# One decoder layer on one core: the first head's inputs loaded at once, the norm vector spread by TensorE, first products taken by kind, statistics on ScalarE alone

## The chip, the cores and the metric

The kernel runs on one core of a Trainium2 chip. The metric is the device time of one execution in microseconds, lower is better. A time is the median of several executions; the profile shows one execution more.

## What is computed

One layer of a hybrid decoder in fp32: 16 meta tokens ahead of 1024 tokens of width 1024, a norm, one projection into the inputs of two head groups (differential attention and a gated recurrence), an output projection, and a feed-forward part with a convolution. Cut to what the change touches:

```python
h = jnp.concatenate([meta, x], axis=1)            # 16 + 1024 rows of 1024
a = rmsnorm(h, ln_mix_pre[l])                     # h * rsqrt(mean(h*h) + eps) * gain
proj = a @ w_in[l]                                # 1024 -> 7 * 512 columns
dq, dk, dv, hq, hf, hi, hg = jnp.split(proj, SPLITS, axis=-1)
y_diff = diff_attention(dq, dk, dv, ...)          # 4 heads
y_hgrn = hgrn2(hq, hf, hi, hg, ...)               # 4 heads
mix = jnp.concatenate([y_diff, y_hgrn], axis=-1) @ w_out[l]
h = h + rmsnorm(mix, ln_mix_post[l])
h = h + rmsnorm(conv_ffn(rmsnorm(h, ln_ffn_pre[l]), ...), ln_ffn_post[l])
```

## The kernel before

**Tiling.** The 1040 rows are nine blocks: block 0 holds the 16 meta rows, blocks 1 to 8 hold 128 rows each. Three blocks make a group; group 0 is blocks 0 to 2 (272 rows), groups 1 and 2 have 384 rows. Each block is cut into two halves of 512 columns (half 0 and 1), which are the first and last four of the eight contraction steps of the projection.

**A product in three passes.** Each fp32 operand is split into a rounded high part and the rest: the activations into `ahi` and `alo`, the weights into `wh` and `wl`. A product of one contraction step is three matmuls, `wh`·`ahi`, `wh`·`alo`, `wl`·`ahi` (`proj_step`, lines 222, 224, 226), into one PSUM bank. `dq`, `dk` and `dv` are the three weight tiles of the first attention head; their results are `pi_dq`, `pi_dk`, `pi_dv`. dv's two weight halves are split into tiles that the rows call `w` (VectorE's cast and GpSimd's rest lie in one tile).

**The path of a block.** `load_x` loads `xt`. `pre_stat` gets the sum of squares with a Square and its accumulator, then Ln and Exp on ScalarE make the factor `ss`. `pre_scale` multiplies one half by `ss` and the gain `gb` on VectorE into `xs`. `pre_turn` turns it with four transposes on TensorE into PSUM (`px`). `pre_hi` casts `px` into `ahi` on ScalarE, `pre_lo` subtracts on VectorE into `alo`. `weights` splits a weight half (`wr`): a cast on ScalarE into `wh`, a subtraction on GpSimd into `wl`. In the profile all of ScalarE's and VectorE's operations carry line 53, that of the wrapper `Ordered`; tile names tell them apart.

**Order.** TensorE's queue is in the order of the code. While `state["ordered"]` is true ScalarE and VectorE keep the code's order too; after that a scheduler orders them. The loads go through one queue, SP's. A tile's readers and writers wait for each other through semaphores per tile: two halves in one tile are one thing to these waits. PSUM tiles have a tag: `ip` and `m` have two banks each, `S` has two tiles of two banks. `interleave` feeds a stretch of products with pieces of side work, here the blocks 3 to 5 (`pre_blocks`), which belong to group 1, between the products of group 0; `lead` and `fill` set how many products (counted in ns) go between the pieces.

**The front before.** `gb`'s first half is made by a matmul with a row of ones and copied; its second half is loaded with the row repeated for every partition. Statistics of block 0 are VectorE's, their squares go to PSUM (`pj`). Group 0's products begin as soon as half 0 of the three blocks is cast, each contraction step with all three kinds. `dv`'s weights are loaded when buffers come free. `pi_dv` takes a bank of `ip`, which `pi_dq` and `pi_dk` have had.

Of the kernel before, what the change touches and what calls it, by code (L numbers as in the profile page):

```python
# [13 lines left out]
ALU = mybir.AluOpType  # L14
# [71 lines left out]
def layer_kernel(ctx: ExitStack, tc: tile.TileContext, x, meta, table, lbl, gpre, gpost, win,  # L86
# [148 lines left out]
    xts = {}  # L235

    def load_x(i):
        xts[i] = zp.tile([P, D], F32, tag="xt", name=f"xt{i}", bufs=4)
# [12 lines left out]

    def pre_scale(i, half, ss, xs):
        r = rows(i)
        cs = slice(512 * half, 512 * half + 512)
        V.scalar_tensor_tensor(xs[:r, :512], xts[i][:r, cs], ss[:r], gb[:r, cs], ALU.mult, ALU.mult)

    def pre_turn(i, half, xs, pt=None):
        r = rows(i)
        pt = ps_m(f"px{i}_{half}") if pt is None else pt
        for j in range(4):  # L260
            T.transpose(pt[:, j * r:(j + 1) * r], xs[:r, P * j: P * (j + 1)], ident[:r, :r])
# [494 lines left out]
    parts = []  # L756
    grow = zp.tile([P, D], F32, tag="xt", name="grow", bufs=4)[:1]
# [5 lines left out]
    def load_raw(m, c, name):  # L763
        raw = wp.tile([P, 512], F32, tag="wr", name=f"wr_{name}_{c}", bufs=3)
        SY.dma_start(raw, win[m][:, 512 * c: 512 * (c + 1)])
        return raw

    def split_raw(raw, name):
        hi = wp.tile([P, 512], F32R, tag="wh", name=f"wh_{name}", bufs=4)
        lo = wp.tile([P, 512], F32R, tag="wl", name=f"wl_{name}", bufs=4)  # L770
        split(hi, lo, raw)
        return hi, lo

    raws = {}
# [6 lines left out]
    stat = {0: pre_stat(0)}  # L781
    pt = ps_m("pg")
    T.matmul(pt, ones, grow[:, :512], start=True, stop=True)
    V.tensor_copy(gb[:, :512], pt)
    load_x(3)
    xss = {}
    for i in range(3):
        for half in range(2):
            if i < 2 and half == 1:
                xss[i, 1] = xss[i, 0][:, 512:]  # L790
            elif i < 2:
                xss[i, 0] = zp.tile([P, D], F32, tag="xs", name=f"xs{i}")
            else:
                xss[i, half] = ap_.tile([P, 4, P], F32, tag="at0", name=f"xs{i}_{half}", bufs=2).rearrange("p a c -> p (a c)")
    parts = [[None, None], [None, None]]

    def weights(j, c):
        parts[j][c] = split_raw(raws[j, c], f"{tiles[j][1]}_{c}")

    def scale(i, half):  # L800
        pre_scale(i, half, stat[i], xss[i, half])

    spare = {}

    def turn(i, half):
        if i and i not in spare:
            spare[i] = ps_s(f"px{i}")
        return pre_turn(i, half, xss[i, half], spare[i][:, half] if i else None)

    stat[1] = pre_stat(1)  # L810
    scale(0, 0)
    h00 = turn(0, 0)
    stat[2] = pre_stat(2)
    scale(1, 0)
    h10 = turn(1, 0)
    scale(0, 1)
    h01 = turn(0, 1)
    pre_hi(*h00)
    weights(0, 0)
    raws[1, 1] = load_raw(tiles[1][0], 1, tiles[1][1])  # L820
    load_x(4)
    scale(2, 0)
    h20 = turn(2, 0)
    pre_lo(*h00)
    pre_hi(*h10)
    scale(1, 1)
    h11 = turn(1, 1)
    load_x(5)
    pre_lo(*h10)
    pre_hi(*h20)  # L830
    weights(1, 0)
    scale(2, 1)
    pre_lo(*h20)
    pre_hi(*h01)
    pre_lo(*h01)
    weights(0, 1)
    pre_hi(*h11)
    pre_lo(*h11)
    for i in range(3):
        xts.pop(i)  # L840

    def head0_first():
# [4 lines left out]
        for half in range(2):  # L847
            for j in range(2):
                for k in range(4 * half, 4 * half + 4):
                    yield from proj_step(pts[j], parts[j], k, t0, t1, lambda: tiles[j][2](0, *g0, t0, t1, pts[j]))  # L850
        yield from proj_group(0, parts[2], tiles[2][1], tiles[2][2])

    first_group = head0_first()
    for _ in range(3):
        next(first_group)
    h21 = turn(2, 1)
    last_hi = pre_hi(*h21)
    last_lo = pre_lo(*h21)
    weights(1, 1)
    state["ordered"] = False  # L860
    third = [ap_.tile([P, 4, 512], F32R, tag="pb", name=f"w3{c}", bufs=2) for c in range(2)]
    parts.append([])
# [715 lines left out]
```

## Time and profile before

| | |
|---|---|
| median of 3 runs | 1347.83 us (1342.91 to 1348.17) |
| the profiled execution | 1345.7 us, its span 1343.9 us |
| TensorE busy | 1290.4 us (96%) |
| VectorE, ScalarE, GpSimd busy | 910.7, 690.6, 429.7 us |
| loads and stores | 165.26 MB, mean 123 GB/s |

A row of the timeline is: start, duration, engine, line, operation, out<-in, shape, count, and in brackets the idle time ahead of it with what ended it. Times of start are counted from the span's start. A row of a stretch is: its ends, its length, then busy time and count of TensorE, its weight loads, VectorE, ScalarE and GpSimd, the granted TensorE clock, the share of the DMA engines, and GB/s.

### The profile page before, as it was taken

The numbers are of one execution on the slowest core, as the hardware profiler recorded it, in microseconds if no ns is written. First come the engines' busy times: TensorE is split into PE (matmuls) and PEld (weight loads), VectorE is DVE, ScalarE is ACT, GpSimd is POOL, SyncE is SP. The second block draws the span as 40 slices with busy tenths as digits, with TensorE's granted clock in tenths as the row PEclk, the third lists the DMA queues.
The fourth block names the chain that finished last, engine by engine and source line by source line (L and its number), as shares of the span: only waits on it lengthen the run. The fifth ranks groups of instructions, "written<-read, shape, count | busy, mean of one in ns | idle before, by whom it ended". The sixth has DMA issues, their size and how long they took to land.

```text
span 1343.9 us, 26160 instructions
## 1 busy us (share of the span) xinstructions
PE 1290.4 (96%) x10170; PEld 1189.0 (88%) x10170; DVE 910.7 (68%) x1535; ACT 690.6 (51%) x1631; POOL 429.7 (32%) x334
## 2 busy tenths in 40 slices
PE   6999999999999998999999999999999999999997
PEld 5899899989999998687899999999999998888875
DVE  7665647574756474636798777787777776697586
ACT  7465356535754666236674444454454444454453
POOL 3211211121102110326046657657656640010121
PEclk9999999999999999999999999999999999999999
DMA  6342334143311223667512222223222225965263
GB/s 214 109 135 67 115 110 150 64 139 117 127 48 53 79 87 114 201 184 251 204 48 87 87 79 80 80 86 104 80 87 77 74 89 187 340 192 159 92 203 118
DMA packets 99570, 165.26 MB, mean 123 GB/s; under 512 B 10051, under 2 KB 34915, under 8 KB 99446
## 3 DMA queue, kind: packets, MB, share of 16 engines
q1 hardware_dynamic: 99446, 163.58, 37.1%
q8 instruction: 80, 1.31, 0.4%
q14 instruction: 44, 0.36, 0.1%
HBM read 122.91 MB, written 40.63 MB: 122 GB/s over the span
## 4 chain that ended last, share of the span: by engine, by line
PE 47%; DVE 5%; DMA 3%; ACT 3%; issue 3%; POOL 2%; SPq 0%; DVEq 0%; ACTq 0%; POOLq 0%
PE pd L1424 5%; PE pd L1423 5%; PE pd L1425 5%; PE pb L1265 4%; PE pb L1266 4%; PE pb L1267 4%; PE pc L1265 2%; PE pa L1265 2%; PE pc L1267 2%; PE pa L1267 2%; PE pa L1266 2%; PE pc L1266 2%; PE py L945 1%; PE py L941 1%; PE py L943 1%
## 5 line engine op out<-in xcount | busy, mean ns | idle before, releaser
L1265 PE MATMUL pb<-t,uh 128*128 128x258 f32 x504 | 143.8, 285 | 5.7 <-DVE u L53 5.7
L1266 PE MATMUL pb<-t,uh 128*128 128x258 f32 x504 | 142.6, 283 | 0.0
L1267 PE MATMUL pb<-t,ul 128*128 128x258 f32 x504 | 142.3, 282 | 0.0
L1424 PE MATMUL pd<-wl,gh 128*128 128x512 f32 x308 | 121.9, 396 | 0.1
L1423 PE MATMUL pd<-wh,gh 128*128 128x512 f32 x308 | 121.7, 395 | 0.0
L1425 PE MATMUL pd<-wh,gl 128*128 128x512 f32 x308 | 121.7, 395 | 0.0
L53 DVE SCALAR_TENSOR_TENSOR c<-uu,cwt,c 128x514 f32<-128x514 f32 (+1 forms) x88 | 96.8, 1100 | 20.6 <-ACT c L53 19.9
L1232 POOL TENSOR_TENSOR c<-c,c 128x514 f32<-128x514 f32 (+1 forms) x44 | 63.5, 1443 | 121.9 <-ACT c L53 119.2
L1265 PEld LDWEIGHTS pb<-t,uh 128*128 128x128 f32 x504 | 96.1, 191 | 7.1 <-DVE u L53 6.9
L1266 PEld LDWEIGHTS pb<-t,uh 128*128 128x128 f32 x504 | 96.1, 191 | 0.0
L1267 PEld LDWEIGHTS pb<-t,ul 128*128 128x128 f32 x504 | 95.9, 190 | 0.0
L1265 PE MATMUL pa<-t,uh 128*128 128x258 f32 (+1 forms) x336 | 95.3, 284 | 0.0
L1266 PE MATMUL pa<-t,uh 128*128 128x258 f32 (+1 forms) x336 | 95.1, 283 | 0.0
L1267 PE MATMUL pa<-t,ul 128*128 128x258 f32 (+1 forms) x336 | 95.0, 283 | 0.0
L1265 PE MATMUL pc<-t,uh 128*128 128x258 f32 (+1 forms) x336 | 94.0, 280 | 0.0
L1267 PE MATMUL pc<-t,ul 128*128 128x258 f32 (+1 forms) x336 | 93.9, 280 | 0.0
L1266 PE MATMUL pc<-t,uh 128*128 128x258 f32 (+1 forms) x336 | 93.7, 279 | 0.0
L53 DVE SCALAR_TENSOR_TENSOR c<-ug,cwt,c 128x514 f32<-128x514 f32 (+1 forms) x88 | 86.1, 978 | 2.7 <-ACT c L53 2.0
L147 POOL TENSOR_TENSOR ul<-ws,uh 128x512 fp32r<-128x512 f32 x42 | 61.1, 1454 | 42.8 <-ACT uh L53 38.3
L1424 PEld LDWEIGHTS pd<-wl,gh 128*128 128x128 f32 x308 | 57.7, 187 | 14.9 <-DVE wl L53 0.9
L1425 PEld LDWEIGHTS pd<-wh,gl 128*128 128x128 f32 x308 | 57.7, 187 | 14.1
L1423 PEld LDWEIGHTS pd<-wh,gh 128*128 128x128 f32 x308 | 57.7, 187 | 14.1
(349 smaller groups left out, 4131.1 us busy)
## 6 DMA issues: line engine op xcount, KB each, us to landing
ra<-in_wup_dram SPq DMA_DIRECT2D x88, 256.0 KB, 2.7
mp<-msc SPq DMA_DIRECT2D x23, 512.0 KB, 5.4
wd<-in_wdown_dram SPq DMA_DIRECT2D x44, 256.0 KB, 4.4
tsc<-wd SPq DMA_DIRECT2D x44, 256.0 KB, 3.2
wi<-tsc SPq DMA_DIRECT2D x44, 256.0 KB, 2.8
gi<-gsc SPq DMA_DIRECT2D x33, 256.0 KB, 4.2
wi<-in_wdown_dram SPq DMA_DIRECT2D x33, 256.0 KB, 3.0
gsc<-c SPq DMA_DIRECT2D x22, 257.0 KB, 2.1
```

Source lines behind the costliest of these rows:

```text
L53: ins = call(*args, **kw)
L147: (eng or G).tensor_tensor(lo, raw, hi.bitcast(F32), op=ALU.subtract)
L941: T.matmul(py[:r], mh, hi, start=(first and k == ks[0]), stop=False)
L943: T.matmul(py[:r], mh, lo, start=False, stop=False)
L945: T.matmul(py[:r], ml, hi, start=False, stop=(last and k == ks[-1]))
L1232: G.tensor_tensor(cg, cg, cu, op=ALU.mult)
L1265: T.matmul(pt, hi[:, s], th[:, k], start=(first and k == 0), stop=False, skip_group_check=True)
L1266: T.matmul(pt, hi[:, s], tl[:, k], start=False, stop=False, skip_group_check=True)
L1267: T.matmul(pt, lo[:, s], th[:, k], start=False, stop=(k == 3), skip_group_check=True)
L1423: T.matmul(py, gh[:, s], wh, start=(k == 0 and pr not in (3, 7)), stop=False, skip_group_check=True)
L1424: T.matmul(py, gh[:, s], wl, start=False, stop=False, skip_group_check=True)
L1425: T.matmul(py, gl[:, s], wh, start=False, stop=(k == NH - 1), skip_group_check=True)
```

## The change

All is in the first stretch of the program.

- **Loads.** All of the first head's inputs are issued at once, ahead of any wait for a buffer: three tiles that are first used much later (`X0`, `X1`, `X2`) take blocks 2 to 5, the fourth half of dq and dk and both halves of dv. `gb`'s repeated load is gone: the whole row is loaded once.
- **Norm vector.** Both halves of `gb` are made by a matmul with ones and a copy.
- **Statistics.** ScalarE squares all blocks, block 0 too; the squares go to `xs` in SBUF instead of PSUM, and `xs` is then overwritten by the scaling.
- **Turns.** Blocks 1 to 8 have both halves in one two-bank `S` tile (before, blocks 3 to 8 had a bank of `m` for each half).
- **Products by kind.** `head0_first` takes the products of dq and dk kind by kind: four steps of `wh`·`ahi` for dq, four for dk, then `wl`·`ahi`, `wh`·`alo`, and so on. `pi_dv` takes a bank of `m`.
- **Interleaving.** `interleave(first_group, ..., 800, 3500)` becomes `(450, 4900)`.

```diff
     def pre_stat(i):
         r = rows(i)
-        junk = ps_s(f"pj{i}").rearrange("p a c -> p (a c)")
+        xss[i] = zp.tile([P, D], F32, tag="xs", name=f"xs{i}", bufs=3)
         ss = zp.tile([P, 1], F32, tag="ss", name=f"ss{i}", bufs=3)
-        if i == 0:
-            V.scalar_tensor_tensor(junk[:r], xts[i][:r], 1.0, xts[i][:r], ALU.mult, ALU.mult, accum_out=ss[:r])
-        else:
-            A.activation(junk[:r], xts[i][:r], AF.Square, accum_out=ss[:r])
+        A.activation(xss[i][:r], xts[i][:r], AF.Square, accum_out=ss[:r])
         rstd_of(ss[:r], ss[:r], D)
...
     def pre_block(i):
         with tc.issue_after(last_hi.ins):
             ss = pre_stat(i)
-        xs = zp.tile([P, D], F32, tag="xs", name=f"xs{i}")
         for half in range(2):
-            pre_scale(i, half, ss, xs[:, 512 * half:])
-        xts.pop(i)
+            pre_scale(i, half, ss)
+        pt = ps_s(f"px{i}")
         for half in range(2):
-            out_ = pre_turn(i, half, xs[:, 512 * half:])
+            out_ = pre_turn(i, half, pt[:, half])
             pre_hi(*out_)
             pre_lo(*out_)
             yield
...
-    SY.dma_start(grow[:, :512], gpre[:, :512])
-    for i in range(3):
-        load_x(i)
-    SY.dma_start(gb[:, 512:], gpre[:, 512:].to_broadcast([P, 512]))
+    SY.dma_start(grow, gpre)
+    spare = [spare_tile(t) for t in ("X1", "X2", "X0")]
+    load_x(0)
+    load_x(1)
+    load_x(2, spare[2][:, :D])
...
     for c in range(2):
         for j in range(2):
-            if (j, c) != (1, 1):
-                raws[j, c] = load_raw(tiles[j][0], c, tiles[j][1])
+            load_raw(j, c)
+    load_x(3, spare[1][:, :D])
+    for c in range(2):
+        load_raw(2, c)
+    load_x(4, spare[1][:, D:2 * D])
+    load_x(5, spare[2][:, D:2 * D])
...
+    for half in range(2):
+        cs = slice(512 * half, 512 * half + 512)
+        pt = ps_m(f"pg{half}")
+        T.matmul(pt, ones, grow[:, cs], start=True, stop=True)
+        V.tensor_copy(gb[:, cs], pt)
+        if half == 0:
+            pre_scale(0, 0, stat[0])
...
+        yield from part(0, 0, 0, ahi, True)
+        yield from part(1, 0, 0, ahi, True)
+        yield from part(0, 0, 1, ahi)
+        yield from part(0, 0, 0, alo)
...
+        pts.append(ps_m("pi_dv0_0")[:, :n])
...
-    interleave(first_group, [pre_blocks([3, 4, 5])], 800, 3500)
+    interleave(first_group, [pre_blocks([3, 4, 5])], 450, 4900)
```

What it moves is seen in the order of the instructions. First, the start of TensorE's queue. Before (`px_173` is block 1, `px_194` block 2, `px_0_162` and `px_1_179` the two halves of block 0):

```order
L783 MATMUL pg<-grow,ones 128x512
L261 MATMUL px_0_162<-ident,xs_152 128x16 x4
L261 MATMUL px_173<-ident,xs_153 128x128 x4
L261 MATMUL px_1_179<-ident,xs_152 128x16 x4
L261 MATMUL px_194<-ident,xs_0_154 128x128 x4
L261 MATMUL px_173<-ident,xs_153 128x128 x4
L222 MATMUL pi_dq_0_224<-ahi,wh_dq_0_185 128x272
L224 MATMUL pi_dq_0_224<-alo,wh_dq_0_185 128x272
L226 MATMUL pi_dq_0_224<-ahi,wl_dq_0_186 128x272
L261 MATMUL px_194<-ident,xs_1_155 128x128 x4
```

And now (`px_175` is block 1, `px_176` block 2):

```order
L796 MATMUL pg_164<-grow,ones 128x512
L796 MATMUL pg_168<-grow,ones 128x512
L261 MATMUL px_0_173<-ident,xs_149 128x16 x4
L261 MATMUL px_175<-ident,xs_154 128x128 x8
L261 MATMUL px_176<-ident,xs_159 128x128 x8
L837 MATMUL pi_dq_0_228<-ahi,wh_dq_0_204 128x272 x4
L837 MATMUL pi_dk_0_229<-ahi,wh_dk_0_212 128x272 x2
L261 MATMUL px_1_174<-ident,xs_149 128x16 x4
L837 MATMUL pi_dk_0_229<-ahi,wh_dk_0_212 128x272 x2
L837 MATMUL pi_dq_0_228<-ahi,wl_dq_0_205 128x272 x4
L837 MATMUL pi_dq_0_228<-alo,wh_dq_0_204 128x272 x4
```

The second norm product and the wide turns of both halves have moved ahead of the first product, and eight products with high parts alone stand ahead of the first with `alo`.

Second, TensorE's queue in the dv products, with the semaphores that a row waits for (DVE, Activation, PE and Pool are those of VectorE, ScalarE, TensorE and GpSimd). Now (`px_311` is block 3, `px_341` block 4; the second group of each name is half 1):

```order
L222 MATMUL pi_dv_0_302<-ahi,w_244 128x272 [waits DVE_49,PE_49]
L261 MATMUL px_311<-ident,xs_304 128x128 [waits DVE_49,PE_49]
...
L261 MATMUL px_311<-ident,xs_304 128x128 [waits DVE_49]
...
L261 MATMUL px_341<-ident,xs_334 128x128 [waits PE_49,Activation_49]
...
L261 MATMUL px_341<-ident,xs_334 128x128 [waits DVE_49]
```

Before, with the halves of block 4 in tiles of their own (`px_0_336` and `px_1_351`):

```order
L261 MATMUL px_0_336<-ident,xs_333 128x128 x4
L222 MATMUL pi_dv_0_343<-ahi,w_239 128x272
L224 MATMUL pi_dv_0_343<-alo,w_239 128x272
L226 MATMUL pi_dv_0_343<-ahi,w_239 128x272
...
L261 MATMUL px_1_351<-ident,xs_333 128x128 x4
L224 MATMUL pi_dv_0_343<-alo,w_239 128x272
```

All six groups of turns of blocks 3 to 5 now stand between dv's products, four apart, where before the first of them stood among dq's and dk's and the later ones seven apart; and the second half of a block is turned into the tile from which VectorE reads the first half for `alo`.

Third, ScalarE around the evacuation of `pi_dq` and `pi_dk` (`q`, `k`). Before, with `px_0_288` and `px_1_306` block 3:

```order
L53 CAST ahi<-px_0_288 128x4x128
L53 ACTIVATE q_0_120<-pi_dq_0_224 64x272
L53 ACTIVATE pj_439,ss_440<-xt_326 128x1024
L53 CAST ahi<-px_1_306 128x4x128
L53 ACTIVATE q_0_121<-pi_dq_0_224 64x272
L53 CAST k_0_122<-pi_dk_0_225 64x272
L53 CAST ahi<-px_0_336 128x4x128
```

And now:

```order
L53 ACTIVATE q_0_120<-pi_dq_0_228 64x272
L53 ACTIVATE xs_362,ss_363<-X_in 128x1024
L53 CAST k_0_122<-pi_dk_0_229 64x272
L53 ACTIVATE q_0_121<-pi_dq_0_228 64x272
L53 CAST ahi<-px_311 128x4x128
L53 ACTIVATE ss_363<-ss_363,eps 128x1
```

Block 3's first cast now comes behind the evacuations and a Square, where before it came ahead of them.

More of the change, by code (lines that the diff above doesn't have):

```diff
@@ L787, in layer_kernel @@
-    for i in range(3):
-        for half in range(2):
[L789 to L798, printed above, removed]
@@ L831, in layer_kernel, with turn @@
+    turned = {}
+    def turn(i, half):
+        turned[i, half] = pre_turn(i, half, banks0[i][half])
+    for i in (1, 2):
+        for half in range(2):
+            pre_scale(i, half, stat[i])
+    pre_scale(0, 1, stat[0])
+    for i, half in ((0, 0), (1, 0), (1, 1), (2, 0), (2, 1)):
+        turn(i, half)
+    pre_hi(*turned[0, 0])
+    pre_hi(*turned[1, 0])
+    weights(0, 0)
+    pre_hi(*turned[2, 0])
+    for i in range(3):
+        pre_lo(*turned[i, 0])
     weights(1, 0)
-    scale(2, 1)
@@ L833, in layer_kernel @@
-    pre_lo(*h20)
-    pre_hi(*h01)
-    pre_lo(*h01)
+    pre_hi(*turned[1, 1])
     weights(0, 1)
[L837 to L840, printed above, removed]
+    last_hi = pre_hi(*turned[2, 1])
+    weights(1, 1)
+    load_x(7)
     def head0_first():
@@ L846, in head0_first, with part @@
         pts = [ps_in(f"pi_{tiles[j][1]}_0")[:, :n] for j in range(2)]
[L847 to L851, printed above, removed]
+        def part(j, half, w, a, first=False, last=False):
+            for k in range(4 * half, 4 * half + 4):
+                T.matmul(pts[j], parts[j][half][w][:, P * (k % 4): P * (k % 4 + 1)], a[:, k, t0:t1],
+                         start=(first and k == 0), stop=(last and k == KD - 1))
+                if last and k == KD - 1:
+                    tiles[j][2](0, *g0, t0, t1, pts[j])
+                yield 115
@@ L853, in layer_kernel @@
+        pts.append(ps_m("pi_dv0_0")[:, :n])
+        for k in range(KD):
+            yield from proj_step(pts[2], parts[2], k, t0, t1, lambda: tiles[2][2](0, *g0, t0, t1, pts[2]))
     first_group = head0_first()
-    for _ in range(3):
+    for _ in range(6):
         next(first_group)
[L856 to L859, printed above, removed]
+    turn(0, 1)
+    pre_hi(*turned[0, 1])
+    for i in range(3):
+        last_lo = pre_lo(*turned[i, 1])
     state["ordered"] = False
```

106 lines of the change are left out of this document (45 added, 61 removed).

## The prediction

> **What bounds the kernel now.** I read the busy times of the page, then a table of stretches cut where TensorE starts and stops waiting, then the timelines of the first 33 us.
>
> ```profile
> span 1343.9 us, 26160 instructions
> PE 1290.4 (96%) x10170; PEld 1189.0 (88%) x10170; DVE 910.7 (68%) x1535; ACT 690.6 (51%) x1631; POOL 429.7 (32%) x334
> ```
>
> TensorE is busy 96% of the span, so only a stretch in which it idles or runs slowly can give time back. The stretches (TensorE's busy time comes first behind the length):
>
> ```profile
> 2.18:11.48 9.30, 6.13 (x23) 3.61 (x23) 5.51 (x9) 5.53 (x15) 3.61 (x6) 1.00 0.87 286
> 11.48:24.55 13.07, 9.73 (x62) 9.04 (x62) 9.55 (x13) 9.16 (x23) 7.32 (x6) 1.00 0.58 191
> 24.55:32.68 8.13, 5.60 (x44) 4.92 (x42) 7.87 (x18) 7.38 (x21) 0.00 (x0) 1.00 0.74 245
> 32.68:49.13 16.45, 16.45 (x100) 15.50 (x101) 10.40 (x27) 7.85 (x19) 0.00 (x0) 1.00 0.01 2
> ```
>
> From 32.68 us TensorE runs 16.45 us without a gap. The change ends ahead of there: what it is worth is how much earlier that unbroken run begins. TensorE's timeline before it:
>
> ```profile
> 2.18 2.04 PE L783 MATMUL pg<-grow,ones 1*128 1x512 f32 x2 [2.18 <-DMA grow<-in_gpre_dram]
> ...
> 7.71 1.11 PE L261 MATMUL px<-ident,xs 128*128 128x128 f32 x4 [1.08 <-DVE xs L53]
> ...
> 11.48 0.60 PE L222 MATMUL pi_dq<-ahi,wh_dq 128*128 128x272 f32 x1
> 14.49 0.60 PE L224 MATMUL pi_dq<-alo,wh_dq 128*128 128x272 f32 x1 [2.42 <-DVE alo L53]
> ...
> 15.11 1.06 PE L261 MATMUL px<-ident,xs 128*128 128x128 f32 x4
> 15.82 0.58 PE L222 MATMUL pi_dq<-ahi,wh_dq 128*128 128x272 f32 x1
> ...
> 17.32 0.42 PE L222 MATMUL pi_dq<-ahi,wh_dq 128*128 128x272 f32 x1
> 17.55 0.33 PE L224 MATMUL pi_dq<-alo,wh_dq 128*128 128x272 f32 x1
> 17.72 0.29 PE L226 MATMUL pi_dq<-ahi,wl_dq 128*128 128x272 f32 x1
> 17.84 0.29 PE L222 MATMUL pi_dk<-ahi,wh_dk 128*128 128x272 f32 x1
> ...
> 21.50 0.63 PE L261 MATMUL px<-ident,xs 128*128 128x128 f32 x4 [0.72 <-DVE xs L53]
> ...
> 24.55 0.60 PE L261 MATMUL px<-ident,xs 128*128 128x128 f32 x4
> 26.85 0.37 PE L222 MATMUL pi_dv<-ahi,w 128*128 128x272 f32 x1 [1.71 <-DVE q L53]
> 27.05 0.29 PE L224 MATMUL pi_dv<-alo,w 128*128 128x272 f32 x1
> ...
> 31.95 0.44 PE L222 MATMUL pi_dq<-ahi,wh_dq 128*128 128x384 f32 x1 [0.54 <-ACT ahi L53]
> 32.68 0.44 PE L224 MATMUL pi_dq<-alo,wh_dq 128*128 128x384 f32 x1 [0.28 <-DVE alo L53]
> 32.95 0.34 PE L226 MATMUL pi_dq<-ahi,wl_dq 128*128 128x384 f32 x1
> 33.13 0.34 PE L222 MATMUL pi_dq<-ahi,wh_dq 128*128 128x384 f32 x1
> ```
>
> Three losses are to be seen. The second product waits until 14.49 for alo. Products start 0.23 us apart up to 17.55 and 0.12 apart from 17.72, so TensorE is slow at first; it sped up 3.06 us after its unbroken run began at 14.49 (the table's clock column reads 1.00 throughout and does not show it). And dv waits 1.71 us for its bank, which dq holds. Taking 0.17 us for the product at 31.95, the unbroken run in effect begins at 32.5.
>
> **The change part by part.** The rows that price the start, on ScalarE, VectorE, GpSimd and the load queue:
>
> ```profile
> 4.60 0.29 ACT L53 ACTIVATE ss<-ss,eps 16x1 f32<-16x1 f32 x1 [2.59 <-DVE pj L53]
> ...
> 5.16 1.03 ACT L53 ACTIVATE pj<-xt 128x1024 f32<-128x1024 f32 x1
> 6.12 0.19 ACT L53 ACTIVATION_READ_ACCUMULATOR pj<-xt 128x1 f32 x1
> ...
> 6.78 1.01 ACT L53 ACTIVATE pj<-xt 128x1024 f32<-128x1024 f32 x1
> ...
> 8.87 0.62 ACT L53 CAST wh_dq<-wr_dq 128x512 fp32r<-128x512 f32 x1 [0.30 <-DMA wr_dq<-in_win_dram]
> 9.39 0.58 ACT L53 CAST ahi<-px 128x512 fp32r<-128x512 f32 x1
> ...
> 22.16 0.59 ACT L53 CAST ahi<-px 128x512 fp32r<-128x512 f32 x1 [0.70 <-PE px L261]
> ```
>
> ```profile
> 3.22 1.22 DVE L53 SCALAR_TENSOR_TENSOR pj<-xt 16x1024 f32<-16x1024 f32 x1 [3.22 <-DMA xt<-in_meta_dram]
> 4.37 0.67 DVE L53 COPY gb<-pg 128x512 f32<-128x512 f32 x1
> ...
> 8.23 1.40 DVE L53 SCALAR_TENSOR_TENSOR xs<-xt,ss,gb 16x512 f32<-16x512 f32 x2 [0.57 <-DMA gb<-in_gpre_dram]
> ...
> 11.76 0.69 DVE L53 TENSOR_TENSOR alo<-px,ahi 128x512 fp32r<-128x512 f32 x1 [1.34 <-PE px L261]
> ...
> 19.49 1.20 DVE L53 CAST w<-wr 128x512 fp32r<-128x512 f32 x1 [0.46 <-DMA wr<-in_win_dram]
> 20.61 3.10 DVE L53 SCALAR_TENSOR_TENSOR xs<-xt,ss,gb 128x512 f32<-128x512 f32 x3
> ...
> 24.82 1.41 DVE L53 SCALAR_TENSOR_TENSOR xs<-xt,ss,gb 128x512 f32<-128x512 f32 x2
> ```
>
> ```profile
> 12.02 1.27 POOL L147 TENSOR_TENSOR wl_dk<-wr_dk,wh_dk 128x512 fp32r<-128x512 f32 x1 [0.46 <-ACT wh_dk L53]
> ```
>
> ```profile
> 11.58 0.33 SPq L765 DMA_DIRECT2D wr_dk<-in_win_dram  x1
> ```
>
> *Statistics on ScalarE.* The meta rows are there at 3.2. A Square and its read take about 1.2, so the first Ln starts at 4.4 instead of 4.60, and with 1.62 a block (5.16 to 6.78) block 2's factor is there at 8.15, 0.3 us sooner. A Square into SBUF has no row here; the casts bound its extra cost between 0 and 0.04 (0.58 out of PSUM, 0.62 out of SBUF). I take 0. The Trainium skill, page "ScalarE: Activation LUTs", section "Step-by-step: what each stage is for", speaks against this edit: ScalarE writes PSUM sooner than SBUF; it gives no figure, and no run here shows the pair.
>
> *Norm vector by TensorE.* A second product adds 2.04 us on TensorE (to 6.2), its copy 0.67 on VectorE: block 1's first scaling starts at 6.85 (6.91 before). The 256 KB broadcast load and the 0.57 us wait for it go. Nothing gained or lost beyond 0.1.
>
> *Scalings and turns.* Five scalings 0.7 apart end at 7.6, 8.3, 8.95, 9.6 and 10.3. A slow group of four turns takes 0.71 and a tail of 0.35, so block 1's pair is done at 9.2 and block 2's at 10.65. Both halves of a block share one tile now, and the first cast waits for both (the row at 11.76 shows such a wait). Block 2's cast ends at 11.25 and the first product starts at 11.3, against 11.48. Six more casts of 0.5 end at 13.9.
>
> *Products by kind.* The first twelve use block halves and high parts that are there, so the wait of 2.42 goes. GpSimd's four low parts, 1.27 each from 10.3, end at 11.6, 13.0, 14.3 and 15.6, each ahead of its turn. Slow for 3.06 us, to 14.4: twelve products and the four narrow turns. Then 36 at 0.126 are 4.5: dq and dk end at 18.9, against 24.55. That is 5.6 us ahead.
>
> *Loads at once.* The fourth weight half was issued at 11.58 and dv's halves landed as late as 19.49; now their issues stand among the first eleven on the queue, about 0.47 apart (the first eleven are out by about 6 us), and they are wanted at 13.2 and later. That wait is covered; without the cover it costs 0.5 to 1.5.
>
> *What comes late next.* dv gets a free bank, so the 1.71 goes. But TensorE's queue now holds the second half's turns of blocks 3 to 5 behind the first half's alo, since both write one tile. ScalarE reaches the casts behind Squares (1.06 each) and the evacuations of q and k. In that order, with the rows' durations: VectorE casts dv's halves to 16.5 and scales block 3 beside GpSimd to 19.0 (1.0 each, as at 20.61); turns 3a 19.0; ScalarE's q, Square, k and q push cast 3a to 20.0 and alo to 21.5; turns 3b at 21.55. Cast 3b at 22.2, turns 4a 22.4; a Square and k come ahead of cast 4a (24.0), alo ends 25.3; turns 4b 25.35. Turns 5a 26.2; lg and a Square ahead of cast 5a (27.6), small VectorE work ahead of alo, which ends at 28.9; turns 5b 28.95, three products, and group 1 starts at 29.7. Nine handovers between engines at 0.05 (0.03 from the end of the turns at 21.50 to the cast at 22.16; I take a little more) make that 30.2. Three idle stretches of about 2 us give back 3.3 of the 5.6.
>
> *Sum.* 32.5 − 30.2 = 2.3 us, rounded to 2.2 for the Squares' 0.04 each. Behind the front each engine's order is as before, and TensorE has no slack until 49.13, so the gain stays. The profiled execution took 1345.7 us (its span of 1343.9 and 1.8 around it); by it the result is 1343.5. The runs' median is 1347.83, 2.1 above; I place the result about half way between the two readings, 1343.5 and 1345.6, at **1344.5**.
>
> **The rivals.** *The clock comes late.* 3.06 us is one sample; if TensorE speeds up only at 17.5, as it did before, 1.4 of the gain goes (14 products at 0.1). Worse, it may fall back in the three idles: after 2.42 us of idle (12.07 to 14.49) it was slow, after 1.71 still fast (0.29 for the product at 27.05). An idle near 2.1 lies between. From the second idle on, 11 products at 0.1 and three groups of turns at 0.45 cost 2.4, and 3.06 us of group 1 at half rate 1.5: 3.9 in all, or **1.7 slower than before, 1347.4** by the profiled execution and 1349.5 by the median. It decides at an idle of 1.7 to 2.4 us. The Trainium skill, page "TensorE: Matmul & The Clock Gate", section "Part 1: The HAM clock gate (the "warmup" mystery)", states a free-running window of about 3.4 us for both directions; by that the speed-up would lie between 14.7 and 18.1, and one idle of 2 us alone would not drop it. The trace's 3.06 is close to the page's figure.
>
> *The clock comes early.* The second norm product keeps TensorE at work from 2.2 to 6.2 without a break (before, to 4.2), and the four wide turns follow closely. If it is fast from there on, the turns take 0.45 less a group (0.60 with its tail at 24.55 against 1.06 at 15.11), the first product comes 0.6 sooner and dk's last ends near 17.5, behind GpSimd's low parts; q and the chain behind it start 1.3 sooner. That is 1.3 to 2 more: about 4 faster, 1341.7 by the profiled execution. Against it: the wide turns from 7.71 to 11.5 did not make it fast before.
>
> *Loads crowd.* Fourteen loads without the earlier waits could delay x's block 2 or the first weight half. The stretch to 11.48 moved 286 GB/s with the broadcast among them; one load late by 1 us shifts all behind it by 1, which leaves a gain of 1.2: 1344.5 by the profiled execution.
>
> **How the numbers follow.** Forecast 0.58, clock late or lost 0.20, clock early 0.12, crowding 0.06, something outside the first 60 us 0.04. 0.5% is 6.7 us, about what a measurement of this kernel can tell from no change; no case in the front reaches it, only the spread of the runs (1342.91 to 1348.17) put on top, and the last case. Faster by more 0.08, within 0.86, slower by more 0.06. The range runs from the early clock on a low run (1340) to the lost clock on a high one (1349.5).
>
> **What would show it.** Right: first product near 11.3, no wait before the last dk product near 19, three TensorE idles of about 2 us before turns of px released by VectorE's alo, group 1 from about 30, then no gap for 16 us. Wrong: no such idles, products 0.23 apart behind 18, a load among the releasers before 15 us, or a run from group 1 on whose gaps differ from before.

## The result and the profile after

The changed kernel takes 1344.53 us (median of 20 runs, 1337.81 to 1354.11) against 1346.71 us before (20 runs, 1339.65 to 1350.41). The ratio is 0.9994, with a 95% interval of 0.9978 to 1.001: no difference that can be measured. Four executions of later runs (one of own_tile, two of own_early, one of own_early_2) took 1789 to 3429 us and are left out of the ratios. The profiled execution took 1337.81 us. Its page begins:

```profile
span 1335.9 us, 26155 instructions
PE 1288.3 (96%) x10172; PEld 1187.0 (89%) x10172; DVE 909.4 (68%) x1534; ACT 692.6 (52%) x1633; POOL 426.3 (32%) x334
```

TensorE's timeline of the changed kernel, the rows that answer to those of before:

```profile
7.82 3.67 PE L261 MATMUL px<-ident,xs 128*128 128x128 f32 x16 [1.11 <-DVE xs L53]
12.17 0.77 PE L837 MATMUL pi_dq<-ahi,wh_dq 128*128 128x272 f32 x4 [0.68 <-ACT ahi L53]
...
18.36 0.67 PE L837 MATMUL pi_dk<-ahi,wl_dk 128*128 128x272 f32 x4
18.86 0.29 PE L222 MATMUL pi_dv<-ahi,w 128*128 128x272 f32 x1
18.98 0.62 PE L261 MATMUL px<-ident,xs 128*128 128x128 f32 x4
...
23.38 1.11 PE L261 MATMUL px<-ident,xs 128*128 128x128 f32 x4 [3.28 <-DVE alo L53]
...
27.96 1.12 PE L261 MATMUL px<-ident,xs 128*128 128x128 f32 x4 [0.80 <-DVE alo L53]
...
32.24 0.73 PE L261 MATMUL px<-ident,xs 128*128 128x128 f32 x4 [0.49 <-DVE alo L53]
...
33.19 0.34 PE L222 MATMUL pi_dq<-ahi,wh_dq 128*128 128x384 f32 x1
...
67.30 0.39 PE L222 MATMUL pi_hf<-ahi,wh_hf 128*128 128x272 f32 x1 [1.31 <-ACT k L53]
```

Up to 18.86 us the change does what it says: dq and dk are done and dv begins without a wait, where before the last turns ahead of dv stood at 24.55 and dv itself began at 26.85. Then all of it is given back. TensorE stands still for 3.28 us, until VectorE has taken alo of block 3's first half, and comes back slow (1.11 us for four turns against 0.62); the clock column, read in steps of 0.1 us, falls to 0.50 at 22.2, inside this wait, and is back at 32.4. Group 1 starts at 33.19, later than before (32.5 in effect). The first product of the next weights, pi_hf, stood at 66.75 before, behind a wait of the same 1.31 us; it now stands at 67.30. So this execution is 0.55 us *later* at 67 us and yet 8.0 us shorter in its span. Those 8.5 us arose behind 67 us, which the edit does not reach; single executions of one kernel spread over 16 us (1337.81 to 1354.11), and this one is the lowest of its kernel. Part of them can be the clock's: in the profile of before it was halved three times more, for 3.41 us each (from 181, 536 and 772 us), in this one not once between 32.4 and 1329 us, and 3.41 us at half rate cost at most 1.7.

The table of stretches, for the time up to dv and for that behind it (the granted clock stands ahead of the DMA share):

```profile
11.30:18.90 7.60, 6.92 (x54) 6.56 (x53) 4.73 (x9) 6.99 (x17) 6.80 (x6) 1.00 1.04 396
18.90:30.20 11.30, 7.22 (x36) 6.66 (x36) 10.27 (x19) 7.07 (x19) 1.09 (x1) 0.65 0.27 85
```

In the second one TensorE runs 36 instructions at a mean clock of 0.65, and VectorE is the busy engine: 10.27 of 11.30 us. VectorE's and GpSimd's timelines show why alo came so late:

```profile
17.31 3.23 DVE L53 SCALAR_TENSOR_TENSOR xs<-X_in,ss,gb 128x512 f32<-128x512 f32 x2 [0.18 <-ACT ss L53]
20.57 0.43 DVE L53 SCALAR_TENSOR_TENSOR q<-pi_dq,q 64x272 fp32r<-64x272 f32 x1
...
22.65 0.67 DVE L53 TENSOR_TENSOR alo<-px,ahi 128x512 fp32r<-128x512 f32 x1
```

```profile
16.87 3.12 POOL L871 TENSOR_TENSOR w<-X_in,w 128x512 fp32r<-128x512 f32 x2 [0.36 <-DVE w L53]
```

Block 3's two scalings take 1.6 us each while GpSimd takes dv's low parts, itself at 1.56 instead of 1.27. q's evacuation waits behind them, ScalarE's cast of block 3 behind q, and alo behind the cast.

### The profile page after: what moved, and what is told of

Same layout as the page of the kernel before. It is cut to its first block, busy times and chain, and to the rows that moved or that the text cites. A ratio compares the mean times of both kernels' runs of the same rounds, so it can differ in the third digit from the quotient of the medians.

```text
span 1335.9 us, 26155 instructions
## 1 busy us (share of the span) xinstructions
PE 1288.3 (96%) x10172; PEld 1187.0 (89%) x10172; DVE 909.4 (68%) x1534; ACT 692.6 (52%) x1633; POOL 426.3 (32%) x334
## 3 DMA queue, kind: packets, MB, share of 16 engines
q8 instruction: 80, 1.31, 0.4%
## 4 chain that ended last, share of the span: by engine, by line
PE 47%; DVE 5%; ACT 3%; issue 3%; DMA 2%; POOL 2%; SPq 0%; DVEq 0%; POOLq 0%; ACTq 0%
PE pd L1427 5%; PE pd L1428 5%; PE pd L1426 5%; PE pb L1268 4%; PE pb L1270 4%; PE pb L1269 4%; PE pc L1268 2%; PE pc L1269 2%; PE pa L1268 2%; PE pa L1270 2%; PE pc L1270 2%; PE pa L1269 2%; PE py L948 1%; PE py L944 1%; PE py L946 1%
```

## The experiments

Letters name the theories in the expectations. **Theory (A):** the gain is lost behind 18.9 us, by a wait for alo that the shared tile makes, by VectorE's crowding beside GpSimd, and by the clock that falls in the idle. **Rivals:** the fall was a chance (B); VectorE's and ScalarE's own work holds the front, whatever the tiles (C); the front does not matter to the rest (D); and some for single runs.

The marks of every profile. "Rise" and "fall" are read from the trace's record of the granted clock. The record begins at the rise (the clock column reads 1.00 ahead of it); from there products are 0.13 us apart instead of 0.23. "Fall" is where the clock is halved ahead of group 1. The expectations were written with the rise as the spacing showed it, 12.2 to 12.4 where the record has 11.0 to 12.1.

| kernel | rise | fall | longest idle 18.9 us to group 1 | group 1 | pi_hf | ratio to before (95%) |
|---|---|---|---|---|---|---|
| before | 17.6 | none | 1.71 | 32.5 | 66.75 | 1 |
| changed | 12.0 | 22.2 | 3.28 | 33.19 | 67.30 | 0.9994 (0.9978–1.001) |
| again | 11.0 | 28.0 | 3.27 | 32.05 | 66.79 | 1.0003 (0.9985–1.0021) |
| own_tile | 12.1 | 25.7 | 1.56 | 29.73 | 63.91 | 0.9986 (0.9971–1.0002) |
| filler | 16.9 | none | 1.49 | 32.98 | 67.12 | 1.0022 (1.0006–1.0037) |
| low_vec | 16.2 | none | 2.45 | 32.67 | 66.56 | 1.0 (0.998–1.0019) |
| by_k | 11.5 | 25.2 | 3.33 | 33.27 | 67.09 | 1.0013 (0.9991–1.0034) |
| stats_old | 11.1 | 28.1 | 3.23 | 32.56 | 67.73 | 0.9996 (0.9976–1.0016) |
| own_early | 11.6 | none | 0.82 | 27.35 | 61.88 | 0.998 (0.996–0.9999) |
| own_early_2 | 16.9 | none | 0.91 | 29.51 | 64.42 | 0.9969 (0.995–0.9989) |
| own_early_l | 16.3 | none | 2.06 | 30.16 | 64.27 | 0.9987 (0.9971–1.0003) |
| early_shared | 16.2 | none | 2.01 | 32.03 | 66.40 | 0.9985 (0.9972–0.9997) |
| own_warm | 10.5 | 24.1 | 2.21 | 28.41 | 62.87 | 0.9965 (0.9949–0.9981) |
| best | 11.6 | none | 0.82 | 27.35 | 62.22 | 0.9974 (0.9957–0.9992) |

**again:** the changed kernel once more.

> The changed kernel as it is, a second profile. Theory (A): the gain at the first products is given back where the turns of the second half of block 3 wait for VectorE's alo of the first half, and the idle there drops TensorE's clock. By (A) the marks repeat: first product 12.1 to 12.3 us, dv's first 18.8 to 19.0, an idle of 3.0 to 3.5 before the second turns of block 3, products 0.22 apart behind it, group 1 from 33.0 to 33.4. Rival (B), that the lower clock was a chance of that one execution: the same idle, products 0.12 to 0.13 apart behind it, group 1 from 31.0 to 32.0. The total lies in 1338 to 1354 by either; pi_hf's first product of the next stage, which stood at 67.30, lies within 0.3 of it by (A) and near 65.5 by (B).

Measured, TensorE's timeline:

```profile
23.14 0.66 PE L261 MATMUL px<-ident,xs 128*128 128x128 f32 x4 [3.27 <-DVE alo L53]
...
27.27 0.66 PE L261 MATMUL px<-ident,xs 128*128 128x128 f32 x4 [2.02 <-DVE alo L53]
...
28.44 1.06 PE L261 MATMUL px<-ident,xs 128*128 128x128 f32 x4
...
32.05 0.34 PE L222 MATMUL pi_dq<-ahi,wh_dq 128*128 128x384 f32 x1
```

The idle of 3.27 repeats, and the clock falls again, but 6 us later: the turns at 23.14 and 27.27 are still fast, and it falls at 28.0 with TensorE at work. Neither (A) nor (B) said that. Group 1 comes at 32.05 where (A) said 33.0 at the earliest. pi_hf is at 66.79, within 0.04 of before, and the span is 1340.5: the same front gives spans 4.6 us apart.

**own_tile:** second halves get a tile of their own.

```diff
-        pt = ps_s(f"px{i}")
         for half in range(2):
-            out_ = pre_turn(i, half, pt[:, half])
+            out_ = pre_turn(i, half, ps_s(f"px{i}_{half}")[:, half])
```

> The second halves of blocks 3 to 5 (and 6 to 8) are turned into a tile of their own. (A): the second turns of block 3 start once VectorE has scaled the half, at 20.6 instead of 23.38; TensorE then waits before block 4's turns for alo of 3a, 1 to 2 us, which leaves the clock up; group 1 from 29.0 to 30.5, 2.5 to 4 sooner than 33.19. Rival (C), that VectorE's and ScalarE's own work on the blocks and not the shared tile holds the front: turns come sooner but group 1 not before 31.5. Rival (D), that the front's end hardly matters to the rest: pi_hf's first product does not move by what group 1 moves. The total follows group 1, 2.5 to 4 us under the changed kernel, inside the spread of the runs.

```profile
20.77 0.63 PE L261 MATMUL px<-ident,xs 128*128 128x128 f32 x4 [0.56 <-DVE xs L53]
...
23.47 0.66 PE L261 MATMUL px<-ident,xs 128*128 128x128 f32 x4 [1.56 <-DVE alo L53]
...
29.73 0.34 PE L222 MATMUL pi_dq<-ahi,wh_dq 128*128 128x384 f32 x1
```

As (A) said, in all but the clock, which fell at 25.7 although no idle was over 1.56. The second turns of block 3 wait for the scaling alone, group 1 is 2.3 us sooner than in the profile of again (32.05), whose clock was also halved once for 3.41 us, and 3.5 sooner than in the changed kernel's first profile, and pi_hf moves by 2.9 against again, so (D) falls. Against (C), group 1 is well ahead of 31.5. In the total the edit is not told from before.

**filler:** products that nothing reads, in the long idle.

```diff
+        pt = ps_m("fill")[:, :272]
+        for k in range(24):
+            T.matmul(pt, parts[0][0][0][:, P * (k % 4): P * (k % 4 + 1)], ahi[:, k % 4, :272], start=True, stop=True)
```

> 24 products whose result nothing reads are put ahead of the second turns of block 3, some 3.0 us of work at the fast pace, in the idle of 3.28. (A): the idle shrinks to 0 to 0.4, the turns start at 23.3 to 23.6 as before, the clock stays up: turns 0.62 to 0.65 for four instead of 1.11, products 0.12 apart instead of 0.22, group 1 from 31.0 to 32.0, that is 1.2 to 2.2 sooner; the later idles of up to 1.7 do not drop it. Rival (E), that the lower clock has another cause than the idle: products 0.22 apart behind 23.4 all the same, group 1 at 33.2 or later.

Inconclusive. The clock stayed up and the idle went, as (A) said, but this execution's clock had also risen late (16.9), all marks stand 2 us later for it, and low_vec below kept its clock without fillers. The kernel is slower by 0.22% although its front is no later than that of the changed kernel; in its profile the excess over again arises mostly between 450 and 600 us (some 5.5 of 8.2). Its clock was halved there for 3.41 us twice, from 539 and from 573 us, and that of again not at all, which is at most 3.4 of them; the rest is left open.

**low_vec:** dv's low parts on VectorE.

```diff
-            G.tensor_tensor(third[c][:, 1], raws[2, c], third[c][:, 0].bitcast(F32), op=ALU.subtract)
+            V.tensor_tensor(third[c][:, 1], raws[2, c], third[c][:, 0].bitcast(F32), op=ALU.subtract)
```

> dv's two low weight parts are taken by VectorE instead of GpSimd, so that nothing runs on GpSimd while VectorE scales block 3. (A): VectorE's scalings of block 3 take 0.70 to 0.78 each instead of 1.6, the low parts 0.65 to 0.75 each; the second half of block 3 is scaled at 20.3 to 20.5 (20.54 before), but the evacuation of q no longer comes behind it, so alo of 3a ends 0.5 to 1.2 sooner than 23.3 and the idle before the second turns of block 3 is 1.5 to 2.6; group 1 at 31 to 32.5. Rival (C), VectorE is full whatever the order: the time moved to it is what the slower scalings cost, and group 1 stays at 33 or later. A scaling that still takes over 1.2 would say that GpSimd was not its cause.

VectorE's timeline, and below it TensorE's:

```profile
16.83 1.28 DVE L53 TENSOR_TENSOR w<-X_in,w 128x512 fp32r<-128x512 f32 x2
20.07 0.43 DVE L53 SCALAR_TENSOR_TENSOR q<-pi_dq,q 64x272 fp32r<-64x272 f32 x1 [1.95 <-ACT q L53]
20.54 1.41 DVE L53 SCALAR_TENSOR_TENSOR xs<-X_in,ss,gb 128x512 f32<-128x512 f32 x2
```

```profile
28.13 0.66 PE L261 MATMUL px<-ident,xs 128*128 128x128 f32 x4 [2.45 <-DVE sub L53]
...
29.12 0.60 PE L261 MATMUL px<-ident,xs 128*128 128x128 f32 x4
```

Without GpSimd beside them the scalings take 0.70 each: GpSimd was the cause of 1.6. But the scheduler now put q ahead of them, and with the late rise (16.2) q came late: VectorE stood idle for 1.95. Group 1 stays at 32.67, between (A) and (C). The idle of 2.45 did not drop the clock.

**by_k:** the products of group 0 in the order of before, each step with its three kinds.

```diff
+        for half in range(2):
+            for j in range(2):
+                for k in range(4 * half, 4 * half + 4):
+                    yield from proj_step(pts[j], parts[j], k, t0, t1, lambda: ...)
```

> The products of the first group go back to the order of before (for each of a half's four k: ahi by wh, alo by wh, ahi by wl), all else as in the changed kernel. The prediction credited the order by kind with the 2.42 us wait. (A): the second product waits 0.6 to 0.9 for alo of block 2, and a later one 0.5 to 1 for alo of the second halves, so dv's first product comes at 19.5 to 20.5 in place of 18.6 to 18.9 where the clock rises as early, and group 1 moves less, 0 to 1, since VectorE's work stands ahead of the turns. Rival (F), that the new order buys nothing once the loads and scalings are early: no wait over 0.5 in dq and dk, dv's first product within 0.4 of the changed kernel's. The total is 0 to 1 us over the changed kernel's.

```profile
12.87 0.39 PE L224 MATMUL pi_dq<-alo,wh_dq 128*128 128x272 f32 x1 [0.33 <-DVE alo L53]
...
19.44 0.29 PE L222 MATMUL pi_dv<-ahi,w 128*128 128x272 f32 x1
```

The wait that was 2.42 us is 0.33. From the first product (12.14) to dv's first it is 7.30 us, against 6.69 in the changed kernel: the order by kind is worth 0.6. That is (F) in size more than (A). The wait had gone because VectorE now scales everything before it takes alo (before, a scaling of 1.46 us at 12.37 stood between its alo's at 11.76 and 13.76). This is read from the two timelines; no run takes it apart. Group 1 does not follow (33.27).

**stats_old:** blocks 0 to 2 with the statistics of before.

```diff
+        if i == 0:
+            V.scalar_tensor_tensor(junk[:r], xts[i][:r], 1.0, xts[i][:r], ALU.mult, ALU.mult, accum_out=ss[:r])
```

> For blocks 0 to 2 the statistics are taken as before: block 0's on VectorE, the Squares of 1 and 2 into PSUM. The prediction gave the edit 0.2 to 0.3 us at block 2's factor and nothing at the first product. (A): Squares into PSUM take 1.01 to 1.03 against 1.04 to 1.06, block 2's factor comes 0 to 0.3 sooner or later, first product within 0.3 of 11.9 to 12.3. Rival: VectorE, which now holds block 0's Square of 1.22 ahead of the copy of gb and the scalings, shifts the first product by 0.5 to 1.2.

First product at 11.97 (11.94 in again), block 2's factor at 8.47 (8.50 there). The edit is worth nothing: a Square into PSUM took 1.01 and 1.03, into SBUF 1.04 to 1.06.

**own_early:** on top of own_tile, the statistics of blocks 3 and 4 and the scalings of block 3 go ahead of dv's casts, GpSimd's low parts behind them, and dv goes by kind.

```diff
+    ss3, ss4 = pre_stat(3), pre_stat(4)
+    for half in range(2):
+        last_lo = pre_scale(3, half, ss3)
     state["ordered"] = False
...
+        for n, (w, a) in enumerate(((0, ahi), (0, alo), (1, ahi))):
+            for half in range(2):
+                yield from part(2, half, w, a, n == 0, n == 2)
```

> On top of the tile of its own for second halves: the statistics of blocks 3 and 4 and the scalings of block 3 are put ahead of the casts of dv's weights, GpSimd's low parts of dv come behind block 3's scalings, and dv's products go by kind so that the low parts are wanted last. (A): block 3's scalings take 0.7 to 0.8 each and end at 17.8 to 18.2 (20.54 in the changed kernel), alo of 3a ends 1.5 to 2.5 sooner than 23.3, idles of TensorE stay under 1.5, group 1 from 26.5 to 28.5, 5 to 6.5 sooner than in the changed kernel, and pi_hf's first product at 60.5 to 62.5. Rival (C), VectorE's sum of work holds the front: group 1 not before 29. Rival (G), GpSimd's low parts slow the later scalings instead, to over 1.2 each: group 1 at 28.5 to 30. The total follows group 1: 4 to 6 us under before.

VectorE and TensorE:

```profile
16.22 1.42 DVE L53 SCALAR_TENSOR_TENSOR xs<-X_in,ss,gb 128x512 f32<-128x512 f32 x2 [0.19 <-ACT ss L53]
17.55 0.76 DVE L53 CAST w<-X_in 128x512 fp32r<-128x512 f32 x2
...
18.81 1.20 DVE L53 SCALAR_TENSOR_TENSOR xs<-X_in,ss,gb 128x512 f32<-128x512 f32 x1
20.04 0.44 DVE L53 SCALAR_TENSOR_TENSOR q<-pi_dq,q 64x272 fp32r<-64x272 f32 x1
...
20.88 1.27 DVE L53 TENSOR_TENSOR alo<-px,ahi 128x512 fp32r<-128x512 f32 x2
```

```profile
21.61 0.66 PE L261 MATMUL px<-ident,xs 128*128 128x128 f32 x4 [0.72 <-DVE alo L53]
...
23.59 0.63 PE L261 MATMUL px<-ident,xs 128*128 128x128 f32 x4 [0.82 <-DVE xs L53]
...
25.55 0.66 PE L261 MATMUL px<-ident,xs 128*128 128x128 f32 x4 [0.82 <-DVE alo L53]
...
27.35 0.33 PE L222 MATMUL pi_dq<-ahi,wh_dq 128*128 128x384 f32 x1
```

(A) in the marks, with block 3 scaled even sooner (17.6). Group 1 is 4.7 us sooner than in again and pi_hf 4.9 sooner than before; (C) falls. Of (G) there is one scaling, that at 18.81: 1.20 beside GpSimd. The ratio to before is 0.998 (0.996 to 0.9999), some 3 us where 4 to 6 were expected.

**own_early_l:** the turns four products earlier, `interleave(..., 450, 4440)`.

> As the kernel with early block 3, and the first turns of block 3 stand four products earlier in TensorE's order, so that each later turn has four products of dv more behind it at the end. (A): cast 3a and all behind it 0.3 to 0.6 sooner; group 1 0 to 0.6 sooner than there, and four more products ahead of it that fill a wait. Rival (C): no change, since VectorE sets the pace, within 0.2.

Group 1 at 30.16, pi_hf at 64.27: with a clock that rose at 16.3 this is to be held against own_early_2 (29.51 and 64.42), where nothing is gained. The scheduler put VectorE's scaling of block 5 behind four alo's, and TensorE waited 2.06 for it.

**early_shared and own_early_2:** the early block 3 with the shared tile, and own_early once more.

> Block 3's early statistics and scalings, GpSimd's low parts behind them and dv by kind as in the kernel with early block 3, but with the shared tile of the changed kernel for a block's two halves. It tells the two causes apart. (A), both cost: block 3 is scaled by 18, so the second turns of block 3 wait for alo of 3a to about 21.5, idle 1 to 2, and two such waits follow: group 1 at 29.5 to 31, between the changed kernel (32.0 to 33.2) and 27.35. Rival (H), the crowding on VectorE alone was the cause and the shared tile costs nothing: group 1 within 0.7 of 27.35. Rival (I), the shared tile alone: group 1 at 32 or later. A late rise of the clock (products 0.23 apart until 16) adds 1 to 2 to each.

> The kernel with own tiles and early block 3 again, for a second profile and twelve more times. (A): group 1 at 27.2 to 27.6 if the clock rises near 12.3, at 28.3 to 30 if near 16.4; pi_hf's first product at 61.5 to 62.2 or 62.8 to 64.5; median 2 to 5 us under the one of before. Rival: the 2.6 us seen were chance, median within 1 of before.

TensorE of early_shared:

```profile
23.35 0.66 PE L261 MATMUL px<-ident,xs 128*128 128x128 f32 x4 [1.57 <-DVE alo L53]
...
27.47 0.66 PE L261 MATMUL px<-ident,xs 128*128 128x128 f32 x4 [2.01 <-DVE alo L53]
...
31.15 0.66 PE L261 MATMUL px<-ident,xs 128*128 128x128 f32 x4 [1.56 <-DVE alo L53]
...
32.03 0.34 PE L222 MATMUL pi_dq<-ahi,wh_dq 128*128 128x384 f32 x1
```

own_early and own_early_2 are one kernel, and differ by 2.16 us at group 1 (27.35, 29.51) with the rise of the clock (11.6, 16.9). Taking that off early_shared, whose clock rose at 16.2, leaves about 29.9 (30.2 if one takes off only what its first dv product is late, 20.55 against 18.70). So from 32.05 the early block 3 gives about 2, the tile of its own 2.3, and both 4.7: two causes of about the same size that add. Only about, since the clock fell in again and in own_tile and not in the other two, and the falls are in these differences. "Early block 3" stands for all that own_early changes beside the tile (statistics, scalings, GpSimd behind them, dv by kind); no run takes these apart. (H) and (I) fall. The median of own_early_2 is 1.85 under before, its ratio 0.9969 (0.995 to 0.9989); with own_early's, two measurements of this kernel lie below 1. How little an interval alone says, early_shared shows: its own also lies below 1 (0.9972 to 0.9997), though its pi_hf is only 0.35 us sooner than before.

**own_warm:** own_early with eleven transposes that nothing reads in TensorE's first waits, and with the work on the small constants put behind block 5, which changes the scheduler's order too.

```diff
+    def keep_busy(n):
+        for _ in range(n):
+            T.transpose(idle[0][:, :P], ident, ident)
```

> As that kernel, with eleven transposes of ident whose results nothing reads in TensorE's waits ahead of the first product (three before the norm products, five before block 1's turns, three behind the last turn), and the small constants' work behind block 5. Ahead of 12 us TensorE was idle 1.06 and 0.68 us there. (A) takes the rise of the clock to need TensorE at work without a break: it comes 3 to 4 us behind the first of them, at 5 to 9 instead of 12.2 or 16.4; wide turns 0.11 apart instead of 0.21, the first product at 11.0 to 11.6, products 0.126 apart from the first, group 1 at 26.3 to 27.3. Rival (J), the rise follows something else than unbroken work: it stays at 12 or later, first product 11.9 to 12.4, group 1 as in the kernel without them (27.35, or 28.3 to 30 with the late rise).

```profile
1.52 0.47 PE L799 MATMUL idle<-ident 128*128 128x128 f32 x1 [1.52 <-POOL ident masks.py:199]
...
7.82 3.23 PE L261 MATMUL px<-ident,xs 128*128 128x128 f32 x16
10.89 0.49 PE L797 MATMUL idle<-ident 128*128 128x128 f32 x3
11.73 0.77 PE L847 MATMUL pi_dq<-ahi,wh_dq 128*128 128x272 f32 x4 [0.35 <-ACT ahi L53]
...
22.83 0.63 PE L261 MATMUL px<-ident,xs 128*128 128x128 f32 x4 [2.21 <-ACT xs L53]
24.09 1.07 PE L261 MATMUL px<-ident,xs 128*128 128x128 f32 x4
```

The clock rose at 10.5, the earliest of all, but 9 us and not 3 to 4 behind the first transpose; neither (A) nor (J) fits. Then ScalarE's new order made TensorE wait 2.21 at 22.83, the clock fell at 24.1, and group 1 came at 28.41. Its median is the lowest of all kernels, 1340.58 against 1345.81, ratio 0.9965 (0.9949 to 0.9981), though group 1 is 1.06 later than in own_early: the front does not explain its place.

**best:** own_warm with block 5's Square behind block 4's factor, block 6's behind block 4's casts, and each scaling behind the alo ahead of its turns.

> The version that the runs point to: own tiles, early block 3, the eleven transposes that read nothing useful in TensorE's early waits, and an order in which ScalarE takes block 5's Square behind block 4's factor (its lead cost the kernel with the transposes a wait of 2.21 us before block 4's turns), block 6's Square behind block 4's casts, and VectorE scales each half just behind the alo that stands before its turns. (A): clock up by 10 to 11.5, first product 11.5 to 11.9, no idle of TensorE over 1.2 between 18 and group 1, so no fall of the clock, group 1 at 26.3 to 27.3 (28.41 with the transposes alone, 27.35 without them), pi_hf's first product at 60.8 to 62. Rival (C), VectorE's sum of work: group 1 not before 27.3. Rival (K), what is put behind block 4 comes late instead: block 6's turns in group 1 wait 0.5 to 1.5, and pi_hf stays at 62 to 63. The median is 4 to 7 us under before; against the kernel with the transposes alone the difference, about 1, is under what the runs can tell.

TensorE's timeline, and the stretch up to group 1 (VectorE's busy time is the third behind the length):

```profile
23.71 0.63 PE L261 MATMUL px<-ident,xs 128*128 128x128 f32 x4 [0.82 <-DVE xs L53]
...
27.35 0.33 PE L222 MATMUL pi_dq<-ahi,wh_dq 128*128 128x384 f32 x1
...
62.22 0.39 PE L222 MATMUL pi_hf<-ahi,wh_hf 128*128 128x272 f32 x1 [2.01 <-ACT k L53]
```

```profile
18.90:27.35 8.45, 6.39 (x50) 5.59 (x49) 8.19 (x19) 7.46 (x18) 2.40 (x2) 1.00 0.36 112
```

The clock rose at 11.6 as in own_early, so the transposes do not bring the rise forward reliably, and the first product came at 12.13, not by 11.9. No idle is over 0.82 and the clock stays up. Group 1 is at 27.35, not sooner than in own_early, as (C) said: VectorE is busy 8.19 of the 8.45 us ahead of it. Of (K) half took place: pi_hf comes at 62.22 behind a wait of 2.01, but block 6's turns did not wait, since TensorE's timeline lists no idle between 27.35 and that wait. The median is 1341.56 against 1344.85, the ratio 0.9974 (0.9957 to 0.9992), some 3 us where 4 to 7 were expected. It is faster than before, as own_warm is; the runs do not tell the two apart, and neither was run beside the changed kernel, whose interval (0.9978 to 1.001) overlaps both of theirs.

## Why the prediction was right, and where its steps were wrong

The forecast, 1344.5 and no measurable difference, is what the 20 runs gave. Its reason was a front 2.2 us shorter, and that did not come: the fronts measured are 0.55 later (changed) and 0.04 later (again) at pi_hf. The change is worth nothing there, and the number came out by luck, because all cases lay within the spread of the runs.

- **Statistics, norm vector, loads:** the norm vector and the loads as predicted within 0.3 (block 1's first scaling at 7.02; no load among the releasers between 6 and 15 us). The first Ln came at 4.40 as worked out, but block 2's factor at 8.58 instead of 8.15: ScalarE waited until 5.27 for block 1's load, so what the first block won was lost. stats_old puts the statistics at 0.0.
- **First product:** 11.3 predicted, 12.17 measured. The mis-sized term is the slow group of turns, put at 0.71 and a tail of 0.35 at the end; sixteen turns take 3.67 with the tail, 0.83 a group, which is most of the difference. They also began 0.2 late (7.82 against 7.6).
- **The clock's rise:** predicted 14.4, measured 12.0 (11.0 in again). By luck this error and that of the first product cancel: dv begins at 18.86, predicted 18.9. Where no transposes were added ahead, this front's clock rose at 11.0 to 12.1 or at 16.2 to 16.9, so a single sample of 3.06 us could not carry this step.
- **Products by kind:** the step gave them the whole 2.42 us wait. by_k shows 0.6; the rest goes with the scalings moved ahead of alo, which the timelines show and no run takes apart.
- **What comes late next:** the place was right (the second turns, released by VectorE's alo, through the shared tile) and own_tile shows it. The size was not: block 3's scalings were put at 1.0 and took 1.6, q, the cast and alo followed later by it, and the first idle was 3.28 in place of about 2. With the clock's fall (next point), this is the step that cost the forecast its gain.
- **The rival "clock comes late, or falls back in the idles"** is what this profile shows: 1.7 later than before was worked out, 0.7 (33.19 against 32.5) measured at group 1. It had 0.20; the fall came in three of three profiles of this front with an early rise (changed, again, stats_old), so it was the likelier case. Its threshold, an idle of 1.7 to 2.4, does not hold: there was no fall after 2.45 (low_vec) and one with no idle over 1.56 (own_tile). The upper end had been read from the slow product at 14.49, when the clock had not yet risen for the first time (17.6). What decides is in the last section.
- **"From group 1 on no gap, the gain stays":** held; pi_hf follows group 1 at 33.8 to 34.9 us in all kernels but stats_old (35.2, its clock halved until 35.0), so what is won at group 1 is still there at pi_hf.

## What to carry to other kernels

Before a stage is shortened, look at the engine that feeds the next one: here VectorE was the busy engine behind 18.9 us, and eight us won by TensorE waited for it. Two halves put in one tile are one thing to the waits, and a tile for each gave 2.3 us at group 1 for a small edit. Where the total scatters by several us, read such an edit at marks in the trace (a first product, an idle, the clock by spacing), and take several profiles before one number of the clock goes into a sum.

## What was not expected of the hardware

- **The clock's rise scatters within one kernel:** 11.6 and 16.9 us in two profiles of own_early, 2.16 us at group 1. With transposes from 1.52 on it came at 10.5 and 11.6. The Trainium skill, page "TensorE: Matmul & The Clock Gate", section "Part 1: The HAM clock gate (the "warmup" mystery)", gives a free-running window of about 3.4 us and says that the rise varies by 0.5 us with it; the scatter here, 5.3 us, is larger than either.
- **The fall does not follow the length of an idle, but the share of a stretch of 3.41 us.** In all 14 traces the recorded clock changes only at whole multiples of 3.413 us from its rise, to within 0.003 us, which agrees with the window that the Trainium skill's page above gives; where this grid lies differs from one execution to the next, also of one kernel. Up to the last 15 us of the kernels the clock was halved 38 times, six of them ahead of group 1, and each time TensorE had been busy for 1.64 us or less of the stretch just ended. Behind every busier stretch it stayed up; of the stretches at 1.64 or less eight (1.47 and up) left it up as well, so the limit lies about there and is not sharp. The stretches of again, and the one of low_vec that holds most of its idle of 2.45 (TensorE's busy time behind the length, the clock third from the end):

```profile
21.21:24.62 3.41, 1.48 (x13) 1.48 (x14) 3.28 (x7) 2.52 (x7) 0.00 (x0) 1.00 0.62 213
24.62:28.03 3.41, 1.39 (x13) 1.18 (x12) 3.31 (x10) 2.28 (x7) 0.00 (x0) 1.00 0.00 0
28.03:31.45 3.42, 2.88 (x15) 2.56 (x14) 3.33 (x13) 2.54 (x7) 0.00 (x0) 0.50 0.02 5
```

```profile
26.43:29.85 3.42, 1.72 (x15) 1.72 (x16) 3.42 (x10) 1.91 (x6) 0.00 (x0) 1.00 0.00 0
```

- **The clock came back, or rose first, at the end of a stretch with about 2.9 us or more of TensorE's work (the least is that of again above), and not with 2.82 or less.** That is where the scatter of the rise comes from: the wait of 0.68 us ahead of the first product lies whole in one stretch, or is cut by its end, or lies behind it. In own_early the stretch to 11.56 had 3.17 us and the clock rose; in own_early_2 the one to 13.49 had 2.74, and it took the next, to 16.90. Stretches filled for the most part with the norm products of one row and narrow turns did not raise it (3.64 to 7.05 in own_warm, busy throughout). Both limits were read off afterwards, from the busy times as the profile models them; no run set out to test them.
- **GpSimd slowed VectorE where all of VectorE's tensors lie in SBUF:** a scaling took 0.70 alone and 1.2 to 1.6 beside GpSimd, while q (0.44) and alo (0.64) out of PSUM took their usual time beside it (own_early, 20.04 and 20.88, GpSimd at work from 18.05 to 21.16). The Trainium skill, page "GPSIMD Engine Reference", section "1. Specifications", names instructions with two SBUF inputs, and those in a 2-port perf mode, as the cases that contend; the scalings agree. A cast from SBUF to SBUF, with one input, was slowed too: 1.20 us at 19.49 in the kernel before, beside GpSimd, where the one at 18.61, with GpSimd all but idle, took 0.43; no run shows which mode it used.
